# Where the embedding's projection waits in SBUF: places for all sixteen tiles, stores after x has landed, squares of x ahead of copies

## The chip, the core and the metric

The kernel runs on one core of a Trainium2 chip. The metric is the device time of one execution in microseconds (us), as the median of several runs. A second source is one profiled execution, of which every instruction's start and duration is known; its own time stands beside its span below.

## What is computed

One layer of a decoder trunk on a sequence of 512 positions and 2048 channels, in float32. Cut to what matters here:

```python
h = rms_norm(x, norm_g)                    # x: (512, 2048)
proj = h @ w_in                            # queries, keys, values, gates, ...
kc = compress(k_c, pe_k, w1_k, w2_k)       # k_c, v_c: slices of proj
vc = compress(v_c, pe_v, w1_v, w2_v)
o_a = attention(q, kc, vc, k_s, v_s, k_w, v_w, gates) * silu(z_a)
o_b = spatial_gating(uv, ...) * silu(z_b)
merged = g_a * (o_a @ w_up_a) + g_b * (o_b @ w_up_b)
x = x + merged @ w_out
x = x + sigmoid(x @ w_ple_gate) * (p @ w_ple)    # p: (512, 256), w_ple: (256, 2048)
return rms_norm(x, final_g)
```

The product `p @ w_ple` depends on nothing else, so the kernel computes it first, while x is on its way, and stores it in DRAM until the last stage. It is "the embedding's projection" of the title.

## The kernel before

All matrix products run through one generator, `gemm()`, over a list of jobs. A float32 matrix is split into a high part (ScalarE, line 98, or line 100 with a scale) and a low part (VectorE, line 104 or 106), and each product is three matmuls: high by high, low by high, high by low. Weights come in loads of 512 KB (`load_to`, line 138, on SyncE's queue) into three rotating buffers `raw`; each load holds two sub-tiles, which are split into `hi` (four buffers) and `lo` (three). A load is issued only when its buffer is free, and everything behind it on SyncE's queue waits with it. `fill(n)` advances the generator by n groups of three matmuls, so the order of each engine's instructions is written out by hand and is the order of the program's lines.

The jobs of interest are the first ones. `pl0` to `pl3` are the projection of the embedding: each has eight groups of three matmuls (two steps of the contraction by four blocks of 128 positions) and gives four banks of PSUM, 128 x 512 each. `evac_ple` copies them to SBUF (ScalarE at line 346 or VectorE at line 348, by a string of letters a and d for each job and block) and stores them to the DRAM tensor `spill` from GpSimd's queue (line 349), 512 KB at a time, through three rotating buffers `ple`. Then come `kc0`, `kc1`, `vc0` and `vc1`: keys and values that will be compressed (matmuls at lines 190 to 192), of which `evac_c` makes the tiles `tokk` and `tokv` (lines 327 and 328 on ScalarE, 331 and 332 on VectorE).

The start of the program (lines 555 to 642) interleaves four things by hand. `keep_busy(10)` issues ten matmuls on the identity matrix (line 576). p is transposed (line 601) and split. The four blocks of x, 1 MB each (`xt`, line 570), get their sum of squares on ScalarE (`stats`, line 579, and a square root, line 580), a reciprocal and a scaling on VectorE (`scale`, lines 583 and 584). Then `turn(k)` transposes the k-th 128 channels of all four blocks on TensorE (line 591), and `turned(k)` splits them into `act_h` and `act_l` (lines 100 and 106), the activation for all products with `w_in`. `fill` calls stand between these steps: the projection's matmuls cover the time until x is ready.

PSUM has eight banks, two for each of the letters g, s, t, o. `pl0` and `pl2` use g, g, s, s; `pl1` and `pl3` use t, t, o, o; `turn(0)` and `turn(1)` use s, `turn(2)` uses g, and `turn(3)` to `turn(5)` use s.

SBUF is given out by pools. `xin` holds x, p and the projection's buffers and closes after the last `turn`. `mid` holds the attention's values (`vt`), gates, compressed keys and the masks `b0`, `c0`, `cm`, which GpSimd makes at lines 650 to 658. `cmp` holds the compression's weights; GpSimd clears the margins of `tokk` and `tokv` (line 665) and then loads the weights (lines 668 to 673). The position terms `pek` and `pev` are transposed on TensorE at line 677, after `finish("kc1")`.

Of the kernel before, what the change touches and what calls it, by code (L numbers as in the profile page):

```python
# [12 lines left out]
F32 = mybir.dt.float32  # L13
F32R = mybir.dt.float32r
# [6 lines left out]
P = 128  # L21
S = 512
D = 2048
TT = S // P
KT = D // P
HEADS = 16
GROUPS = 4
HD = 64
NCMP = 32
# [22 lines left out]
def kernel(ctx: ExitStack, tc: tile.TileContext, x, p, norm_g, w_in,  # L52
                      pe_k, w1_k, w2_k, pe_v, w1_v, w2_v, ln_g, ln_b, sgu_w, sgu_b,
                      w_up_a, w_up_b, w_out, w_ple, w_ple_gate, final_g, out):
    nc = tc.nc
    x, out = x[0], out[0]
    p = p[0, 0]
    norm_g, w_in, ln_g, ln_b, sgu_w, sgu_b = norm_g[0], w_in[0], ln_g[0], ln_b[0], sgu_w[0], sgu_b[0]
    pe_k, w1_k, w2_k, pe_v, w1_v, w2_v = pe_k[0], w1_k[0], w2_k[0], pe_v[0], w1_v[0], w2_v[0]
# [8 lines left out]
    def bank(kind, name):  # L68
        return psum.tile([P, 512], F32, tag=kind, name=name)
# [20 lines left out]
    def flush():  # L90
        todo = list(deferred)
        deferred.clear()
        for f in todo:
            f()
# [39 lines left out]
    def load_to(i):  # L134
        while state["loads"] <= min(i, len(loads) - 1):
            job, k0, n = loads[state["loads"]]
            t = stream.tile([P, n, job.cols], F32, tag="raw", name="raw")
            nc.sync.dma_start(t, job.w[k0 * P:(k0 + n) * P, job.c0:job.c0 + job.cols]
                              .rearrange("(k p) c -> p k c", p=P))
            raw[state["loads"]] = (t, k0)  # L140
            state["loads"] += 1

    def split_to(i, more=1):
        while state["high"] <= min(i + more, len(subs) - 1):
            job, k, n, li = subs[state["high"]]
            t, k0 = raw[li]
            if k >= job.kt - job.tail:
                hi = f_tiles["th"][:, k - job.kt + job.tail:][:, :n]
            else:
                hi = stream.tile([P, n, job.cols], F32R, tag="hi", name="hi", bufs=4)  # L150
            src = t[:, k - k0:k - k0 + n]
            high(hi, src)
            parts[state["high"]] = [hi, None, src]
            state["high"] += 1
        while state["low"] <= min(i, len(subs) - 1):
            job, k, n, li = subs[state["low"]]
            pt = parts[state["low"]]
            if k >= job.kt - job.tail:
                pt[1] = f_tiles["tl"][:, k - job.kt + job.tail:][:, :n]
            else:  # L160
                pt[1] = stream.tile([P, n, job.cols], F32R, tag="lo", name="lo")
            low(*pt)
            state["low"] += 1
            li = subs[state["low"] - 1][3]
            if state["low"] == len(subs) or subs[state["low"]][3] != li:
                load_to(li + 3)
# [61 lines left out]
    def fill(n):  # L228
        for _ in range(n):
            next(run, None)  # L230

    def finish(name):
        while name not in done:
            next(run)
        flush()


    ph_ab = ExitStack()
    mid = ph_ab.enter_context(tc.tile_pool(name="mid", bufs=1))
    ph_o = ExitStack()  # L240
    o32 = None


    def h_act(k):
        return act_h[:, k], act_l[:, k]

    vt = mid.tile([P, 2, TT, GROUPS, 2 * HD], F32R, name="vt")
    gates = mid.tile([P, TT, 48], F32, name="gates")
    kc_h = mid.tile([P, GROUPS, NCMP], F32R, name="kc_h")
    kc_l = mid.tile([P, GROUPS, NCMP], F32R, name="kc_l")  # L250
    vc = mid.tile([P, GROUPS, HD], F32, name="vc")

    def kk(b, g):
        return g * 2 + b
# [81 lines left out]
    pl_in, ple_t = {}, {}  # L336
# [2 lines left out]

    def evac_ple(cg):  # L340
        def f(ps):
            for a in range(0, TT, 2):
                o = pl_in["pool"].tile([P, 2, 512], F32, tag="ple", name="ple", bufs=3)
                for t in (a, a + 1):
                    if "dddd aadd ddaa adad".split()[cg][t] == "a":
                        nc.scalar.copy(o[:, t - a], ps[t])
                    else:
                        nc.vector.tensor_copy(o[:, t - a], ps[t])
                nc.gpsimd.dma_start(spilled(cg)[:, a:a + 2], o)
        return f  # L350

    def spilled(cg):
        return spill[:, 512 * cg:512 * cg + 512].rearrange("(t p) c -> p t c", p=P)
# [200 lines left out]

    with tc.tile_pool(name="xin", bufs=4, side="right") as xin:
        xt = [xin.tile([P, D], F32, tag="xt", name=f"xt{t}") for t in range(TT)]
        pl_in["pool"] = xin
        p_nat = xin.tile([P, TT, 256], F32, name="p_nat", bufs=1)
        pl_in["h"], pl_in["l"] = ob_h[:, 0:2], ob_l[:, 0:2]
        sq = ob_h[:, 4:8].rearrange("p f t -> p (f t)")  # L560
        g_row = xin.tile([KT, P], F32, name="g_row", bufs=1)
        g_col = xin.tile([P, KT], F32, name="g_col", bufs=1)
        st = xin.tile([P, TT, 2], F32, name="st", bufs=1)
        nc.sync.dma_start(p_nat, p.rearrange("(t p) c -> p t c", p=P))
        nc.gpsimd.dma_start(g_row, norm_g.rearrange("(k p) -> k p", p=P))
        load_to(1)
        for t in range(TT):
            if t > 1:
                load_to(t)
            nc.sync.dma_start(xt[t], x[t * P:t * P + P])  # L570
        spin = bank("o", "ps_spin")

        def keep_busy(n):

            for _ in range(n):
                nc.tensor.matmul(spin[:, :P], ident, ident, start=True, stop=True)

        def stats(t):
            nc.scalar.activation(sq, xt[t], AF.Square, accum_out=st[:, t, 0:1])
            nc.scalar.activation(st[:, t, 1:2], st[:, t, 0:1], AF.Sqrt, bias=eps_t, scale=1.0 / D)  # L580

        def scale(t):
            nc.vector.reciprocal(st[:, t, 0:1], st[:, t, 1:2])
            nc.vector.tensor_scalar(out=xt[t], in0=xt[t], scalar1=st[:, t, 0:1], scalar2=None, op0=ALU.mult)

        banks = {}

        def turn(k):
            b = banks[k] = bank("ssgssstotosstoto"[k], "ps_x")
            for t in range(TT):  # L590
                nc.tensor.transpose(b[:, t * P:t * P + P], xt[t][:, k * P:k * P + P], ident)

        def turned(k):
            split(act_h[:, k], act_l[:, k], banks[k], g_col[:, k:k + 1])

        keep_busy(10)
        state["more"] = 0
        for j in range(2):
            b = bank("t", "ps_p")
            for t in range(TT):  # L600
                nc.tensor.transpose(b[:, t * P:t * P + P], p_nat[:, t, j * P:j * P + P], ident)
            split(pl_in["h"][:, j], pl_in["l"][:, j], b)
            split_to(j, 0)
        b = bank("o", "ps_g")
        nc.tensor.transpose(b[:, :KT], g_row, ident[:KT, :KT])
        split_to(3, 0)
        fill(8)
        nc.vector.tensor_copy(g_col, b[:, :KT])
        for t in range(2):
            stats(t)  # L610
            scale(t)
        split_to(5, 0)
        fill(8)
        stats(2)
        scale(2)
        split_to(7, 0)
        fill(8)
        stats(3)
        scale(3)
        split_to(8, 0)  # L620
        fill(3)
        turn(0)
        turn(1)
        turned(0)
        fill(1)
        turn(2)
        turned(1)
        fill(2)
        turn(3)
        turned(2)  # L630
        fill(2)
        for k in range(4, KT):
            turn(k)
            turned(k - 1)
            if k % 4 == 0:
                split_to(8 + k // 4, 0)
            fill(1)
        turned(KT - 1)
        state["more"] = 1
        state["ahead"] = 2  # L640
        fill(2)
        split_to(13)
    orow = ph_o.enter_context(tc.tile_pool(name="orow", bufs=1, side="right"))
    o32 = orow.tile([P, 8, S], F32, name="o32")

# [15 lines left out]
    with tc.tile_pool(name="cmp", bufs=1) as cmp:  # L661
        w1t, w2t, pet = {}, {}, {}
# [2 lines left out]
            nc.gpsimd.memset(tok[n][:, :, :, NCMP:], 0.0)  # L665
        for n, w1, w2, pe in (("k", w1_k, w2_k, pe_k), ("v", w1_v, w2_v, pe_v)):
            w1t[n] = cmp.tile([P, 16, HD], F32, name="w1" + n)
            nc.gpsimd.dma_start(w1t[n], w1.rearrange("l d e -> (l d) e").rearrange("(m p) e -> p m e", p=P))
            w2t[n] = cmp.tile([HD, 2, HD], F32, name="w2" + n)
            pet[n] = cmp.tile([NCMP, 2, HD], F32, name="pe" + n)  # L670
            for i in range(2):
                nc.gpsimd.dma_start(w2t[n][:, i], w2)
                nc.gpsimd.dma_start(pet[n][:, i], pe)
        finish("kc1")
        for n in "kv":
            b = bank("t", "ps_pe")
            nc.tensor.transpose(b[:, :NCMP], pet[n].rearrange("l i d -> l (i d)"), ident[:NCMP, :NCMP])
# [236 lines left out]
    n = len(slots)  # L914
# [40 lines left out]
    with tc.tile_pool(name="mlp", bufs=1) as mlp:  # L955
        vn = mlp.tile([P, TT, 1024], F32, name="vn")
        st = mlp.tile([P, TT, 2, 6], F32, name="bst")
# [87 lines left out]
    for cg in range(4):  # L1045
# [13 lines left out]
        for j in range(4):  # L1059
            k = 4 * cg + j  # L1060
# [3 lines left out]
            h, l = x2_act(k)  # L1064
# [31 lines left out]
```

## Time and profile before

| what | value |
|---|---|
| median of 3 runs | 1661.67 us |
| lowest and highest | 1661.51 and 1663.06 us |
| the profiled execution's own time | 1662.88 us |
| its span, first to last instruction | 1661.2 us |
| around the span | 1.68 us |
| TensorE matmul busy | 1643.5 us, 99% of the span |
| VectorE, ScalarE, GpSimd busy | 45%, 37%, 7% of the span |

A row of the timeline gives start, duration, engine, line, operation, output and inputs, and in brackets how long the engine was idle before it and what released it. PE is TensorE's matmuls and PEld its weight loads, DVE is VectorE, ACT ScalarE, POOL GpSimd, SPq SyncE's queue. Matmuls overlap in their pipeline, so the distance from start to start is their cost, not the duration. A row of the windows gives the length of a stretch, then busy time and count of the engine asked for, the clock that TensorE was granted (1.00 is full), the share of time the DMA engines were busy, and GB/s.

### The profile page before, as it was taken

What the parts mean: (1) busy time and instruction counts of PE and PEld (TensorE: products, weight loads), DVE (VectorE), ACT (ScalarE), POOL (GpSimd) and SP (SyncE); (2) the same over time, 40 slices, a digit from 0 to 9 for tenths busy, and PEclk for the clock granted to TensorE, in tenths of its full rate; (3) what the DMA queues carried; (4) which work ended last, traced back from release to release, by engine and by line L of the source; (5) the groups of instructions that cost most, each with busy time, mean ns of one, the idle gap of its engine ahead of it and who ended that gap; (6) DMA issues with size and microseconds to landing.
All of it is one profiled execution on the core that took longest, in us unless ns stands there. A gap on an engine that the chain in (4) does not pass through costs nothing.

```text
span 1661.2 us, 20583 instructions
## 1 busy us (share of the span) xinstructions
PE 1643.5 (99%) x7841; PEld 1370.3 (82%) x7841; DVE 743.5 (45%) x1486; ACT 612.6 (37%) x1229; POOL 116.9 (7%) x148
## 2 busy tenths in 40 slices
PE   8999999999999999999999999999999999999997
PEld 6878988888888888888888888888888888888886
DVE  5434358888884353343232223223223533333336
ACT  5433346667663332233222222222223422223335
POOL 2100000101110002000000000000000000000101
PEclk9999999999999999999999999999999999999999
DMA  7422421111114333333333333333333522363333
GB/s 291 130 76 74 114 77 52 39 51 51 49 54 140 101 90 89 90 98 96 99 101 90 101 100 91 102 95 96 102 91 100 202 90 89 92 225 90 102 100 128
DMA packets 217250, 168.02 MB, mean 101 GB/s; under 512 B 5040, under 2 KB 191040, under 8 KB 215616
## 3 DMA queue, kind: packets, MB, share of 16 engines
q1 hardware_dynamic: 213472, 151.57, 31.4%
q0 software_dynamic: 3536, 14.79, 2.4%
q8 instruction: 61, 1.00, 0.2%
q14 instruction: 37, 0.30, 0.1%
q10 hardware_dynamic: 144, 0.36, 0.1%
HBM read 158.31 MB, written 8.39 MB: 100 GB/s over the span
## 4 chain that ended last, share of the span: by engine, by line
PE 96%; DVE 2%; ACT 1%; DMA 0%; issue 0%; POOL 0%; DVEq 0%; POOLq 0%; ACTq 0%
PE ps_wo L198 4%; PE ps_ma L190 3%; PE ps_mb L190 3%; PE ps_wo L199 3%; PE ps_mb L191 3%; PE ps_ma L192 3%; PE ps_ma L191 3%; PE ps_wo L200 3%; PE ps_mb L192 3%; PE ps_pg L198 3%; PE ps_pg L200 3%; PE ps_pg L199 3%; PE ps_t L802 2%; PE ps_za L190 2%; PE ps_za L192 2%; PE ps_za L191 2%
## 5 line engine op out<-in xcount | busy, mean ns | idle before, releaser
L104 DVE TENSOR_TENSOR lo<-raw,hi 128x512 fp32r<-128x512 f32 (+1 forms) x536 | 366.6, 687 | 639.1 <-PE ps_mb L192 127.4
L98 ACT CAST hi<-raw 128x512 fp32r<-128x512 f32 (+1 forms) x536 | 328.1, 615 | 723.8 <-PE ps_wo L200 99.0
L198 PE MATMUL ps_wo<-hi,act_h 128*128 128x512 f32 x256 | 101.0, 395 | 0.1
L200 PE MATMUL ps_wo<-hi,act_l 128*128 128x512 f32 x256 | 99.8, 390 | 0.0
L199 PE MATMUL ps_wo<-lo,act_h 128*128 128x512 f32 x256 | 99.7, 390 | 0.0
L190 PE MATMUL ps_ma<-act_h,hi 128*128 128x512 f32 x256 | 99.6, 389 | 0.0
L191 PE MATMUL ps_ma<-act_l,hi 128*128 128x512 f32 x256 | 99.6, 389 | 0.0
L192 PE MATMUL ps_ma<-act_h,lo 128*128 128x512 f32 x256 | 99.6, 389 | 0.0
L190 PE MATMUL ps_mb<-act_h,hi 128*128 128x512 f32 x256 | 99.6, 389 | 0.0
L191 PE MATMUL ps_mb<-act_l,hi 128*128 128x512 f32 x256 | 99.6, 389 | 0.0
L192 PE MATMUL ps_mb<-act_h,lo 128*128 128x512 f32 x256 | 99.6, 389 | 0.0
L98 ACT CAST pth<-ps_t 128x512 fp32r<-128x512 f32 (+1 forms) x88 | 48.0, 546 | 65.6 <-PE ps_t L802 65.3
L763 ACT ACTIVATE prob<-prob,st 128x512 f32<-128x512 f32 (+3 forms) x128 | 70.7, 555 | 4.0 <-DVE st L754 3.8
L453 POOL TENSOR_TENSOR m<-sig,sig 128x512 f32<-128x512 f32 x16 | 27.0, 1690 | 582.3 <-DVE sig L451 464.1
L104 DVE TENSOR_TENSOR ptl<-ps_t,pth 128x512 fp32r<-128x512 f32 (+1 forms) x88 | 56.2, 639 | 21.3 <-ACT pth L98 20.4
L754 DVE CUSTOM_DVE_ANT_0 prob<-ps_s,b 128x512 f32<-128x512 f32 (+3 forms) x128 | 56.3, 486 | 10.1 <-PE ps_s L751 9.8
L200 PEld LDWEIGHTS ps_wo<-hi,act_l 128*128 128x128 f32 x256 | 48.1, 188 | 10.3
L198 PEld LDWEIGHTS ps_wo<-hi,act_h 128*128 128x128 f32 x256 | 48.1, 188 | 10.2 <-DVE sig L451 0.5
L192 PEld LDWEIGHTS ps_ma<-act_h,lo 128*128 128x128 f32 x256 | 48.0, 188 | 10.0
L192 PEld LDWEIGHTS ps_mb<-act_h,lo 128*128 128x128 f32 x256 | 48.0, 188 | 10.0
L190 PEld LDWEIGHTS ps_mb<-act_h,hi 128*128 128x128 f32 x256 | 48.0, 188 | 10.0
L191 PEld LDWEIGHTS ps_ma<-act_l,hi 128*128 128x128 f32 x256 | 48.0, 188 | 10.0
(316 smaller groups left out, 3684.3 us busy)
## 6 DMA issues: line engine op xcount, KB each, us to landing
raw<-in_w_in_dram SPq DMA_DIRECT2D x164, 512.0 KB, 3.5
raw<-in_w_out_dram SPq DMA_DIRECT2D x32, 512.0 KB, 3.6
raw<-in_w_ple_gate_dram SPq DMA_DIRECT2D x32, 512.0 KB, 3.5
raw<-in_w_up_a_dram SPq DMA_DIRECT2D x16, 512.0 KB, 3.7
raw<-in_w_up_b_dram SPq DMA_DIRECT2D x16, 512.0 KB, 3.7
xt<-in_x_dram SPq DMA_DIRECT2D x4, 1024.0 KB, 10.8
spill<-ple POOLq DMA_DIRECT2D x8, 512.0 KB, 5.6
m<-in_x_dram POOLq DMA_DIRECT2D x4, 1024.0 KB, 7.5
```

Of the source, the lines that this page charges most:

```text
L98: nc.scalar.copy(hi, src)
L104: nc.vector.tensor_tensor(out=lo, in0=src, in1=hi.bitcast(F32), op=ALU.subtract)
L190: nc.tensor.matmul(ps, hi[:, j], ah, start=st, stop=False)
L191: nc.tensor.matmul(ps, hi[:, j], al, start=False, stop=False)
L192: nc.tensor.matmul(ps, lo[:, j], ah, start=False, stop=sp)
L198: nc.tensor.matmul(o, ah[:, sl], hi[:, j], start=st, stop=False)
L199: nc.tensor.matmul(o, ah[:, sl], lo[:, j], start=False, stop=False)
L200: nc.tensor.matmul(o, al[:, sl], hi[:, j], start=False, stop=sp)
L453: nc.gpsimd.tensor_tensor(out=merge_tiles["m"][:, f], in0=merge_tiles[0], in1=t, op=ALU.add)
L754: nc.vector.tensor_tensor_reduce(out=pt[:, j * n:j * n + n], in0=o[:, j], in1=b0[:, 512 - n:], scale=-SLOPE[h], scalar=3.0e38, op0=ALU.add ...
L763: nc.scalar.activation(sl, sl, AF.Exp, bias=st[:, 0, j, hh:hh + 1], scale=-1.0, accum_out=st[:, 1, j, hh:hh + 1])
L802: nc.tensor.transpose(b[:, (2 * e + hh) * P:(2 * e + hh + 1) * P], pts[hh][:, c:c + P], ident)
```

## The change

- The projection's result gets one SBUF tile of 128 x 4 x 4 x 512 with a place for every one of the sixteen blocks, where three rotating buffers of two blocks were.
- The stores to `spill` leave `evac_ple`: four of 1 MB each are issued together, after the last group of `pl3`. Ahead of them on GpSimd stands a copy of one column of `st` into a new tile `order`.
- The copies' engines: `pl1` goes from ScalarE, ScalarE, VectorE, VectorE to VectorE for all four blocks; `pl2` from VectorE, VectorE, ScalarE, ScalarE to ScalarE for all four, in the order 2, 3, 0, 1. `pl0` and `pl3` stay.
- `stats(2)` moves ahead of the `fill(8)` of `pl1`, so its squares stand ahead of what follows on ScalarE; `stats(3)` and `scale(3)` move ahead of the `fill(8)` of `pl2`.
- The load of `w_ple` for `pl3` leaves its place ahead of x's last block on SyncE's queue and stands behind it.
- Eight matmuls on the identity where ten were. Of `pl3`, two groups instead of three stand ahead of `turn(0)`, and three instead of two behind `turn(3)`.
- The pool `mid` and its tiles are opened after `xin` is closed.
- The loads of `pek` and `pev` stand ahead of the other compression weights, and their transposes follow `vc0` instead of `kc1`.

```diff
--- before.py
+++ after.py
@@ -236,19 +236,12 @@
 
 
     ph_ab = ExitStack()
-    mid = ph_ab.enter_context(tc.tile_pool(name="mid", bufs=1))
     ph_o = ExitStack()
-    o32 = None
+    mid = o32 = None
 
 
     def h_act(k):
         return act_h[:, k], act_l[:, k]
-
-    vt = mid.tile([P, 2, TT, GROUPS, 2 * HD], F32R, name="vt")
-    gates = mid.tile([P, TT, 48], F32, name="gates")
-    kc_h = mid.tile([P, GROUPS, NCMP], F32R, name="kc_h")
-    kc_l = mid.tile([P, GROUPS, NCMP], F32R, name="kc_l")
-    vc = mid.tile([P, GROUPS, HD], F32, name="vc")
 
     def kk(b, g):
         return g * 2 + b
@@ -339,14 +332,12 @@
 
     def evac_ple(cg):
         def f(ps):
-            for a in range(0, TT, 2):
-                o = pl_in["pool"].tile([P, 2, 512], F32, tag="ple", name="ple", bufs=3)
-                for t in (a, a + 1):
-                    if "dddd aadd ddaa adad".split()[cg][t] == "a":
-                        nc.scalar.copy(o[:, t - a], ps[t])
-                    else:
-                        nc.vector.tensor_copy(o[:, t - a], ps[t])
-                nc.gpsimd.dma_start(spilled(cg)[:, a:a + 2], o)
+            o = pl_in["out"][:, cg]
+            for t in ((0, 1, 2, 3), (2, 3, 0, 1))[cg % 4 == 2]:
+                if "dddd dddd aaaa adad".split()[cg][t] == "a":
+                    nc.scalar.copy(o[:, t], ps[t])
+                else:
+                    nc.vector.tensor_copy(o[:, t], ps[t])
         return f
 
     def spilled(cg):
@@ -554,20 +545,21 @@
 
     with tc.tile_pool(name="xin", bufs=4, side="right") as xin:
         xt = [xin.tile([P, D], F32, tag="xt", name=f"xt{t}") for t in range(TT)]
-        pl_in["pool"] = xin
+        pl_in["out"] = xin.tile([P, 4, TT, 512], F32, name="ple", bufs=1)
         p_nat = xin.tile([P, TT, 256], F32, name="p_nat", bufs=1)
         pl_in["h"], pl_in["l"] = ob_h[:, 0:2], ob_l[:, 0:2]
         sq = ob_h[:, 4:8].rearrange("p f t -> p (f t)")
         g_row = xin.tile([KT, P], F32, name="g_row", bufs=1)
         g_col = xin.tile([P, KT], F32, name="g_col", bufs=1)
         st = xin.tile([P, TT, 2], F32, name="st", bufs=1)
+        order = xin.tile([P, 1], F32, name="order", bufs=1)
         nc.sync.dma_start(p_nat, p.rearrange("(t p) c -> p t c", p=P))
         nc.gpsimd.dma_start(g_row, norm_g.rearrange("(k p) -> k p", p=P))
         load_to(1)
         for t in range(TT):
-            if t > 1:
-                load_to(t)
             nc.sync.dma_start(xt[t], x[t * P:t * P + P])
+            if t == 1:
+                load_to(2)
         spin = bank("o", "ps_spin")
 
         def keep_busy(n):
@@ -593,7 +585,7 @@
         def turned(k):
             split(act_h[:, k], act_l[:, k], banks[k], g_col[:, k:k + 1])
 
-        keep_busy(10)
+        keep_busy(8)
         state["more"] = 0
         for j in range(2):
             b = bank("t", "ps_p")
@@ -610,15 +602,16 @@
             stats(t)
             scale(t)
         split_to(5, 0)
+        stats(2)
         fill(8)
-        stats(2)
         scale(2)
+        stats(3)
         split_to(7, 0)
+        scale(3)
+        nc.gpsimd.tensor_copy(order, st[:, 3, 0:1])
         fill(8)
-        stats(3)
-        scale(3)
         split_to(8, 0)
-        fill(3)
+        fill(2)
         turn(0)
         turn(1)
         turned(0)
@@ -628,7 +621,9 @@
         fill(2)
         turn(3)
         turned(2)
-        fill(2)
+        fill(3)
+        for cg in range(4):
+            nc.gpsimd.dma_start(spilled(cg), pl_in["out"][:, cg])
         for k in range(4, KT):
             turn(k)
             turned(k - 1)
@@ -640,6 +635,12 @@
         state["ahead"] = 2
         fill(2)
         split_to(13)
+    mid = ph_ab.enter_context(tc.tile_pool(name="mid", bufs=1))
+    vt = mid.tile([P, 2, TT, GROUPS, 2 * HD], F32R, name="vt")
+    gates = mid.tile([P, TT, 48], F32, name="gates")
+    kc_h = mid.tile([P, GROUPS, NCMP], F32R, name="kc_h")
+    kc_l = mid.tile([P, GROUPS, NCMP], F32R, name="kc_l")
+    vc = mid.tile([P, GROUPS, HD], F32, name="vc")
     orow = ph_o.enter_context(tc.tile_pool(name="orow", bufs=1, side="right"))
     o32 = orow.tile([P, 8, S], F32, name="o32")
 
@@ -665,13 +666,15 @@
             nc.gpsimd.memset(tok[n][:, :, :, NCMP:], 0.0)
         for n, w1, w2, pe in (("k", w1_k, w2_k, pe_k), ("v", w1_v, w2_v, pe_v)):
             w1t[n] = cmp.tile([P, 16, HD], F32, name="w1" + n)
-            nc.gpsimd.dma_start(w1t[n], w1.rearrange("l d e -> (l d) e").rearrange("(m p) e -> p m e", p=P))
             w2t[n] = cmp.tile([HD, 2, HD], F32, name="w2" + n)
             pet[n] = cmp.tile([NCMP, 2, HD], F32, name="pe" + n)
             for i in range(2):
+                nc.gpsimd.dma_start(pet[n][:, i], pe)
+        for n, w1, w2 in (("k", w1_k, w2_k), ("v", w1_v, w2_v)):
+            nc.gpsimd.dma_start(w1t[n], w1.rearrange("l d e -> (l d) e").rearrange("(m p) e -> p m e", p=P))
+            for i in range(2):
                 nc.gpsimd.dma_start(w2t[n][:, i], w2)
-                nc.gpsimd.dma_start(pet[n][:, i], pe)
-        finish("kc1")
+        finish("vc0")
         for n in "kv":
             b = bank("t", "ps_pe")
             nc.tensor.transpose(b[:, :NCMP], pet[n].rearrange("l i d -> l (i d)"), ident[:NCMP, :NCMP])
```

## The prediction

> **What bounds the kernel now.** I read the page's busy times and chain first, then the chain of waits of the first 90 us, then the timelines of each engine from 17 to 46 us, since all edits lie in the start of the program.
>
> ```profile
> PE 1643.5 (99%) x7841; PEld 1370.3 (82%) x7841; DVE 743.5 (45%) x1486; ACT 612.6 (37%) x1229; POOL 116.9 (7%) x148
> ...
> PE 96%; DVE 2%; ACT 1%; DMA 0%; issue 0%; POOL 0%; DVEq 0%; POOLq 0%; ACTq 0%
> ```
>
> TensorE is the bound: 96% of the chain is its own work. What an edit can bring is TensorE's idle or slow time, and 1661.2 - 1643.5 = 17.7 us is all the idle there is. The chain of the start, in order of time (start, duration, what), leaves TensorE once for long:
>
> ```profile
> 18.24 0.60 ACT ple L346
> ...
> 19.13 7.11 DMA spill<-ple
> 26.32 1.08 ACT ple L346 x2
> 27.40 1.91 ACT ob_h L579 x2
> 29.33 0.30 ACT st L580
> 29.85 1.30 DVE xt L584
> 31.20 1.33 PE ps_x L591 x5
> ```
>
> A store of the projection takes 7.11 us to land; only then is its `ple` buffer free for ScalarE's copies at 26.32; only after them, ScalarE being in order, come the squares of x's last block, then its scaling, then the transpose. TensorE's rows show what that costs, and the windows show the clock beside it (the three figures after TensorE's count are clock, DMA share, GB/s):
>
> ```profile
> 8.64 0.50 PE L199 MATMUL ps_pl<-lo,ob_h 128*128 128x512 f32 x1 [0.30 <-DVE lo L104]
> ...
> 25.55 0.50 PE L199 MATMUL ps_pl<-lo,ob_h 128*128 128x512 f32 x1 [0.32 <-DVE lo L104]
> ...
> 27.51 0.49 PE L591 MATMUL ps_x<-ident,xt 128*128 128x128 f32 x3
> 31.20 1.33 PE L591 MATMUL ps_x<-ident,xt 128*128 128x128 f32 x5 [3.20 <-DVE xt L584]
> ...
> 35.73 0.63 PE L198 MATMUL ps_pl<-hi,ob_h 128*128 128x512 f32 x1
> 36.16 0.63 PE L199 MATMUL ps_pl<-lo,ob_h 128*128 128x512 f32 x1
> ...
> 36.99 0.60 PE L591 MATMUL ps_x<-ident,xt 128*128 128x128 f32 x4
> ...
> 37.90 0.40 PE L200 MATMUL ps_pl<-hi,ob_l 128*128 128x512 f32 x1
> 38.13 0.40 PE L198 MATMUL ps_pl<-hi,ob_h 128*128 128x512 f32 x1
> ...
> 38.82 0.60 PE L591 MATMUL ps_x<-ident,xt 128*128 128x128 f32 x4
> ```
>
> ```profile
> 30.00:31.00 1.00, 0.00 (x0) 0.56 1.07 422
> ...
> 36.50:37.00 0.50, 0.50 (x3) 0.55 0.00 0
> ```
>
> Three transposes of `turn(0)` run, the fourth needs the last block and waits 3.20 us. In that gap the clock falls to half (0.56 over the slice from 30 to 31), and it comes back only at about 36.95 (0.55 over the half slice before 37.00). Between, matmuls stand 0.43 us apart (35.73 to 36.16) where 0.23 is the step at full clock (37.90 to 38.13). So the store's landing is paid twice: once as idle, once as a slow clock.
>
> **The stall, term by term.** (1) Idle at 31.20: 3.20 us. (2) From 31.20 to 36.99 TensorE starts nine transposes and nine matmuls. At full clock a transpose steps by about 0.09 to 0.11 (four from 38.82 take 0.36 to the next instruction), so they are worth 9 x 0.11 + 9 x 0.23 = 3.1 us; they took 5.79, so the clock cost 2.7. (3) Idle of 0.32 at 25.55 on a `lo` of `pl3`, which VectorE made late because its own copies waited for a store; gone with it.
>
> **Does the last block come in time now?** Three things must hold: its data, ScalarE's turn, VectorE's turn.
>
> ```profile
> 4.12 0.47 SPq L570 DMA_DIRECT2D xt<-in_x_dram  x1
> 9.82 0.38 SPq L138 DMA_DIRECT2D raw<-in_w_ple_dram  x1
> 10.24 0.47 SPq L570 DMA_DIRECT2D xt<-in_x_dram  x1
> ```
>
> Time from issue to landing, in the answers on DMA for these three in order, and for the slowest store:
>
> ```profile
> xt<-in_x_dram SPq DMA_DIRECT2D x1, 1024.0 KB, 12.4
> ...
> raw<-in_w_ple_dram SPq DMA_DIRECT2D x1, 512.0 KB, 8.0
> ...
> xt<-in_x_dram SPq DMA_DIRECT2D x1, 1024.0 KB, 11.7
> ...
> spill<-ple POOLq DMA_DIRECT2D x1, 512.0 KB, 9.2
> ```
>
> Before, the third block lands at 16.5, the load for `pl3` at 17.8, the last block at 21.9, slowed by stores that run beside it. The load waits on SyncE's queue for a buffer until 9.82 and holds the last block behind it. Now the last block is issued right behind the third, at about 4.6, and no store runs until its squares are done. At the rate of the load (512 KB in 1.3 us) it lands at 16.5 + 2.6 = 19.1; at worst at the old 21.9. I take 19.1, the rate of the row next to it. The load follows at 20.4 and must be in by ScalarE's split of it, below.
>
> ```profile
> 15.06 1.13 ACT L98 CAST hi<-raw 128x512 fp32r<-128x512 f32 x2
> ...
> 17.64 1.29 DVE L104 TENSOR_TENSOR lo<-raw,hi 128x512 fp32r<-128x512 f32 x2
> 22.22 1.29 DVE L348 COPY ple<-ps_pl 128x512 f32<-128x512 f32 x2 [3.29 <-DMA spill<-ple]
> 23.42 0.15 DVE L583 RECIPROCAL st<-st 128x1 f32<-128x1 f32 x1
> 23.61 1.29 DVE L584 TENSOR_SCALAR xt<-xt,st 128x2048 f32<-128x2048 f32 x1
> ```
>
> ScalarE: free at 16.2, squares of block 2 from 16.5 (squares and root take 27.40 to 29.63, 2.2 us) to 18.7, of block 3 from 19.1 to 21.3, then two `hi` of `pl3`, 1.13, to 22.4. It then stands ready for `pl2`'s four copies. VectorE: `lo` of `pl2` end at 18.9; four copies of `pl1`, which wait for no store now, 2.6, to 21.5; reciprocal and scaling of block 2, 1.45, to 23.0; two `lo` of `pl3`, 1.3, to 24.3; block 3, 1.45, to 25.7. TensorE comes to `turn(0)` at 27.51 less one group (0.7) less the idle of 0.32, 26.5. So 0.8 us is left, and the fourth transpose comes 0.3 later still. If TensorE starts earlier (next part), VectorE's row moves with it, because `pl0`'s copies stand at its head. The old landing at 21.9 would bring `pl3`'s first `lo` and the scaling late by 1 to 1.5 us each, partly after each other: a rival below.
>
> PSUM: `turn(0)` and `turn(1)` now wait for ScalarE's copies of `pl2`'s blocks 2 and 3, which are put first for that. Each ends a copy's time (0.6) after its last matmul, and six matmuls of `pl3` (1.4 us) stand between: nothing. With all sixteen copies without a store to wait for, what is next late is the fifth transpose group, which waited 0.4 for `act_l` and still will.
>
> **The start of the program.**
>
> ```profile
> 1.43 4.64 PE ps_spin L576 x20
> ...
> 5.86 1.22 PE L601 MATMUL ps_p<-ident,p_nat 128*128 128x128 f32 x8
> ...
> 6.68 0.59 ACT L98 CAST ob_h<-ps_p 128x512 fp32r<-128x512 f32 x1 [4.38 <-PE ps_p L601]
> ```
>
> ```profile
> 0.81 0.44 SPq L564 DMA_DIRECT2D p_nat<-in_p_dram  x1
> ...
> p_nat<-in_p_dram SPq DMA_DIRECT2D x1, 512.0 KB, 4.1
> ```
>
> (The first row is the chain's, the others the timelines'.) Ten filler matmuls are twenty rows at 0.21 to 0.23 us, the slow clock's step. Two fewer bring the transposes of p forward by four rows, 0.85, to 5.0, where p is in (0.81 + 4.1 = 4.9). The first four run at the slow step, so ScalarE starts 0.6 earlier, and the projection with it. Before this was worth nothing, the stall swallowed it; now it is on the path: 0.6. Bounds: 0, if the split of the first weights sets the start, and 0.85.
>
> Of the clock the Trainium skill, "TensorE: Matmul & The Clock Gate", section "Part 1: The HAM clock gate", says that it rises only after a window of about 3.4 us in which TensorE was busy, and that the windows run free of the kernel's start. By that rule fewer fillers may leave no whole busy window ahead of the gaps between 7 and 8.6 us, and the estimate by its figure is a rise 3.4 us later, about 1.5 us lost. The trace neither confirms nor denies it for eight fillers; its rise after the stall (5.75 us of work from 31.20) is slower than the rule's least, and prices the rival below.
>
> **What moves off the path.** GpSimd's four stores carry the same 4 MB. The first two go out when `order` has read the last block's reciprocal, about 24; the last at about 32.5, when `pl3` is copied. They run beside the `w_in` loads, as before. The masks of `mid`, and with them the clearing of `tokk`, now wait for all stores and for the last `act_l`:
>
> ```profile
> 54.10 0.16 POOL L665 MEMSET tokk<- 128x64 f32 x1 [10.89 <-DVE act_l L106]
> ...
> 56.02 0.37 ACT L327 COPY tokk<-ps_kc 64x256 f32<-64x256 f32 x1 [1.22 <-PE ps_kc L192]
> ```
>
> The clearing already waited for that `act_l`; the masks, 2 us of GpSimd's work, now stand behind the wait too and push the weight loads 2 us against TensorE's stream, where `pek` and `pev` go first and are needed only after `vc0`, some 20 us later: nothing. ScalarE's copy to `tokk` at 49.0 (56.02 less 7.0) now needs the fourth store landed. At twice the slowest 512 KB, 18.4, it lands at 50.9: at most 1.9 late, with at least one split sub-tile ahead (the program splits up to two ahead; 12 x 0.23 = 2.8 us of TensorE). I take 0.
>
> **The sum.** 3.20 + 2.7 + 0.32 + 0.6 = 6.8. A second count, from the first back-to-back matmul: 95 steps of 0.23 and sixteen transposes from 8.05 reach `turn(4)` at 31.5 to 31.7, where it stood at 38.82: 7.2. I take 7.0. Span 1661.2 - 7.0 = 1654.2, and with the 1.68 us around it 1655.9 for a profiled execution. The runs of before spread from 1661.51 to 1663.06 with the profiled one, 1662.88, at the upper end. If its 1.2 us over the median lies in the length of the slow clock, which is gone now, the median falls to 1655.9; if it is the profile's own cost, to 1654.7. I forecast 1655.5.
>
> **The rivals.**
> (a) The last block is still late, 0.10. For: 0.8 us is a thin margin, and 25.7 rests on five steps. If it lands at 21.9, squares end at 24.1, the first `lo` of `pl3` at 25.4 (1.3 idle) and the scaling at 27.5 (0.5 more): some 1.8 us, no fall of the clock. 1657.3.
> (b) The clock rises late at the start, 0.08. If work counts only from 8.05 and the rise takes the 5.75 us it took after the stall, matmuls step by 0.43 until 13.8: 5.75 x (1 - 0.23/0.43) = 2.7 lost. 1658.2. Against: TensorE is still busy from 1.43 to about 7 without a gap.
> (c) The change does not free the path, 0.04: some wait that the trace of before cannot show holds the squares where they were, and the clock falls again. About 1661.
> (d) Slower, 0.04: kc0's evacuation. ScalarE and VectorE stand in order behind the wait for the fourth store, and no split passes them. Once the prepared sub-tile is used TensorE idles, and beyond about 3 us its clock falls as at 30 us. It loses what is won, and 3.3 more, when the store lands after about 60, 27 us after its issue; then 1665. Against: 9.2 is the longest of eight half-size stores.
>
> **How the numbers follow.** The forecast has 0.74 and its own range is 1654.2 to 1656.8 (the larger sum with the lower start; half of rival (a)'s delay). To hold 8 in 10 the range takes in (a) and reaches to (b): 1653.9 to 1658.2. A measurement of this kernel tells 0.2%, 3.3 us, from no change: faster means under 1658.3. Forecast, (a) and (b) are faster, 0.92, of which 0.01 is taken off for the edge of (b); (c) and that edge give 0.05 within; (d) 0.04 slower.
>
> **What would show it.** Right: no store in the chain of the start; squares of the last block at about 19 to 21.5; a clock of 1.00 in every slice from 26 to 40; no idle before the transposes over 0.5; `turn(4)` near 31.7; from there each row some 7 us earlier than before, with the same gaps. Wrong: a wait of TensorE on `xt` over 1 us, (a); steps of 0.43 in `pl0`, (b); ScalarE's `tokk` waiting for a store, (d).

## The result, and the profile after

The changed kernel takes 1655.7 us (median of 6 runs, 1655.33 to 1657.22) where the kernel before takes 1661.6 (6 runs, 1660.14 to 1663.06): ratio 0.9964, 95% interval 0.9951 to 0.9977, 5.9 us less. The forecast was 1655.5. The profiled execution has a span of 1653.6 us and a time of 1655.33, the shortest of the six. One execution of the kernel before, in the experiments, took 1819.91 us at a mean granted clock of 0.85; it is in no ratio and in no heap below.

The page's busy times, and the chain of waits of the first 60 us (start, duration, what):

```profile
PE 1639.1 (99%) x7837; PEld 1367.1 (83%) x7837; DVE 742.8 (45%) x1486; ACT 612.9 (37%) x1229; POOL 114.0 (7%) x145
```

```profile
1.30 4.97 DMA raw<-in_w_ple_dram
6.29 0.63 ACT hi L98
6.94 0.70 DVE lo L104
7.68 0.50 PE ps_pl L199
...
25.42 0.88 PE ps_x L583 x8
...
31.38 0.69 DVE ple L340
32.07 0.67 DVE act_l L106
32.88 0.63 PE ps_x L583 x4
```

No store is left in it, and no square of x. From 7.68 on it is TensorE's own work up to one short detour over VectorE at 31.38. TensorE's busy time fell too, by 4.4 us: 1.2 of that is the fillers' row (3.42 for 4.64), because there are two fewer and because they step faster towards their end; most of the rest is work that no longer runs at half clock. The timelines show the last block of x in time (ScalarE, VectorE, TensorE):

```profile
19.23 1.93 ACT L571 ACTIVATE ob_h<-xt 128x2048 fp32r<-128x2048 f32 x1
...
23.42 2.25 ACT L338 COPY ple<-ps_pl 128x512 f32<-128x512 f32 x4 [0.81 <-PE ps_pl L200]
```

```profile
17.99 2.48 DVE L340 COPY ple<-ps_pl 128x512 f32<-128x512 f32 x4
20.38 0.15 DVE L575 RECIPROCAL st<-st 128x1 f32<-128x1 f32 x1
...
23.51 1.30 DVE L576 TENSOR_SCALAR xt<-xt,st 128x2048 f32<-128x2048 f32 x1
```

```profile
7.68 0.50 PE L199 MATMUL ps_pl<-lo,ob_h 128*128 128x512 f32 x1 [0.22 <-DVE lo L104]
...
25.26 1.04 PE L583 MATMUL ps_x<-ident,xt 128*128 128x128 f32 x8
...
31.18 0.60 PE L583 MATMUL ps_x<-ident,xt 128*128 128x128 f32 x4
...
32.88 0.63 PE L583 MATMUL ps_x<-ident,xt 128*128 128x128 f32 x4 [0.40 <-DVE act_l L106]
```

The scaling ends at 24.81; the eight transposes of `turn(0)` and `turn(1)` start at 25.26 without a gap. `turn(4)` is at 31.18, where it stood at 38.82: 7.64 us earlier, and the span is 7.6 us shorter, so the rest of the program moved along unchanged. The median gained only 5.9: the profile of before is 1.3 us above its median of 1661.6, and this one is 0.4 below its own. The experiments show what sets these distances.

### The profile page after: what moved, and what is told of

It reads as the page before. It is cut to its first block, busy times and chain, and to the rows that moved or that the text cites. A ratio compares the mean times of both kernels' runs of the same rounds, so it can differ in the third digit from the quotient of the medians.

```text
span 1653.6 us, 20567 instructions
## 1 busy us (share of the span) xinstructions
PE 1639.1 (99%) x7837; PEld 1367.1 (83%) x7837; DVE 742.8 (45%) x1486; ACT 612.9 (37%) x1229; POOL 114.0 (7%) x145
## 4 chain that ended last, share of the span: by engine, by line
PE 97%; DVE 2%; ACT 1%; DMA 0%; issue 0%; DVEq 0%; SPq 0%; ACTq 0%
PE ps_wo L198 4%; PE ps_wo L200 4%; PE ps_mb L191 4%; PE ps_ma L191 4%; PE ps_ma L190 4%; PE ps_mb L192 4%; PE ps_mb L190 4%; PE ps_ma L192 4%; PE ps_wo L199 4%; PE ps_pg L198 3%; PE ps_pg L199 3%; PE ps_pg L200 3%; PE ps_t L805 2%; PE ps_za L190 2%; PE ps_za L192 2%; PE ps_za L191 2%
## 5 line engine op out<-in xcount | busy, mean ns | idle before, releaser
L190 PEld LDWEIGHTS ps_ma<-act_h,hi 128*128 128x128 f32 x256 | 48.1, 188 | 10.0
L191 PEld LDWEIGHTS ps_mb<-act_l,hi 128*128 128x128 f32 x256 | 48.1, 188 | 9.9
```

Source lines behind the costliest of these rows:

```text
L190: nc.tensor.matmul(ps, hi[:, j], ah, start=st, stop=False)
L191: nc.tensor.matmul(ps, hi[:, j], al, start=False, stop=False)
```

## Experiments

**The kernel before, again.** The same program, to read its scatter.

> The kernel before, unchanged, to read its own scatter (1660.1 to 1663.1 in six runs). Theory: the scatter is the length of the half-clock stretch behind the stall, so the runs' mean granted clock falls with their time; a stretch about 3.4 us longer costs about 1.7 us and lowers the mean clock by about 0.001. Rival: the scatter comes from the DMAs, and the mean clock is the same in short and long runs. Either way a median of 1661 to 1662.

Median 1661.56, ratio 0.9999 (0.999 to 1.0008). Together with the runs of before that stood beside three of these groups, 70 executions fall into three heaps: 25 from 1659.7 to 1660.7 (median 1660.2, mean granted clock 0.9986), 38 from 1661.2 to 1662.1 (1661.7, 0.9976), 7 from 1662.9 to 1663.1 (1663.0, 0.9960). The 16 runs of before in the fourth group fall into the same three (5, 5 and 6, from 1659.8 to 1663.2). This execution's profile is of the first heap, 1660.22:

```profile
31.19 0.77 PE L591 MATMUL ps_x<-ident,xt 128*128 128x128 f32 x5 [2.97 <-DVE xt L584]
```

```profile
30.00:31.00 1.00, 0.00 (x0) 1.00 1.11 420
31.00:32.00 1.00, 0.81 (x6) 1.00 1.03 422
```

Nearly the same idle, 2.97 for 3.20, and no fall of the clock (the figure after the count, 1.00). The execution profiled for the prediction, 1662.88, was of the slowest heap. So the scatter is the clock's: the rival, equal clocks in short and long runs, falls.

**Kept busy through the gap.** In the kernel before:

```diff
         fill(3)
+        spin = bank("g", "ps_spin")
+        keep_busy(14)
         turn(0)
```

> The kernel before with 14 extra matmuls on the identity (28 rows of 0.11 us, 3.1 us) in the gap ahead of turn(0), so that TensorE is kept at work while it waits for the last block of x. Theory: the slow steps after the gap are only the clock, and it now stays full: about 2.7 us less than before, 1659, the transposes still released at about 31.2, matmul steps of 0.23 from 31 to 37. Rival: the slow steps come from traffic of the stores or loads at that time; then 1661.6 and steps of 0.43 as before.

Median 1660.1 (1659.72 to 1660.41), ratio 0.999 (0.9981 to 0.9999).

```profile
31.04 0.77 PE L591 MATMUL ps_x<-ident,xt 128*128 128x128 f32 x5 [0.17 <-DVE xt L584]
```

```profile
31.00:32.00 1.00, 0.96 (x7) 1.00 0.98 401
```

The transposes are released as late as before, the clock stays full, and the two slower heaps are gone: all ten runs lie in the first one. The slow steps were the clock alone. Keeping it full is worth 2.8 us against the profiled execution, of which 2.7, as forecast, lie between the release and the fifth transposes (6.65 us for 9.32), but 1.5 at the median. The 1659 that was named took the 2.7 off the median, and is missed by 1.1.

**Places alone.** The kernel before with enough buffers:

```diff
-  o = pl_in["pool"].tile([P, 2, 512], F32, tag="ple", name="ple", bufs=3)
+  o = pl_in["pool"].tile([P, 2, 512], F32, tag="ple", name="ple", bufs=8)
```

The pool `mid` is opened after `xin` for it, since the two don't fit beside each other.

> The kernel before with eight buffers for the projection instead of three (and the pool of values opened after x's is closed, to make room): no copy waits for a store, and nothing else is changed: stores at once, order of squares and copies, loads and ten fillers as before. Theory: ScalarE's two copies of pl2 then wait for TensorE until about 25.9, the last block's scaling ends at about 29.7, and TensorE idles some 1.9 us instead of 3.2; 1.6 us less than before if the clock still falls, 4.3 less if it does not: 1657.3 to 1660. Rival: the wait for the store was all of it; then about 6.3 less, 1655.4, and no idle ahead of the fourth transpose.

Median 1660.27 (1658.43 to 1661.13), ratio 0.9993 (0.9984 to 1.0002): 1.35 less than the runs beside it, not clear of no change, and 0.3 above the range that was named. ScalarE and TensorE:

```profile
24.68 1.27 ACT L340 COPY ple<-ps_pl 128x512 f32<-128x512 f32 x2 [2.27 <-PE ps_pl L200]
25.84 1.92 ACT L573 ACTIVATE ob_h<-xt 128x2048 fp32r<-128x2048 f32 x1
```

```profile
29.75 0.77 PE L585 MATMUL ps_x<-ident,xt 128*128 128x128 f32 x5 [2.06 <-DVE xt L578]
```

The copies wait for no store any more, but for TensorE itself, 2.27 us, and the squares stand behind them. 1.9 us of idle was forecast, 2.06 is left. The rival, that the store was all of it, falls. The clock stays full in this profile, of a run of 1659.29, but not in every run, it seems: the three with a mean clock of 0.997 took 1660.48 to 1661.13, the other seven 1658.43 to 1660.38.

**Squares back behind the copies.** In the changed kernel:

```diff
-        stats(3)
         split_to(7, 0)
-        scale(3)
-        nc.gpsimd.tensor_copy(order, st[:, 3, 0:1])
         fill(8)
+        stats(3)
+        scale(3)
+        nc.gpsimd.tensor_copy(order, st[:, 3, 0:1])
```

> The changed kernel with the squares and scaling of the last block put back behind pl2's four copies. Theory: ScalarE, in order, waits for TensorE's pl2 until 23.4, copies until 25.6, squares until 27.9; scaling ends at about 29.4; TensorE, at turn(0) at about 25.5, idles 3.7 us and the clock may fall again: 3.7 more without the fall, 5.4 to 6.4 more with it, 1659.4 to 1662. Rival: places and deferred stores are what counts, and the order is worth under 1 us: under 1656.7.

Median 1661.26 (1661.12 to 1662.24), ratio to before 1.0002 (0.9993 to 1.0011): 5.6 us are given back, the whole change, and inside the range that was named.

```profile
29.65 1.33 PE L583 MATMUL ps_x<-ident,xt 128*128 128x128 f32 x5 [3.72 <-DVE xt L576]
```

```profile
28.00:29.00 1.00, 0.00 (x0) 0.96 0.00 0
29.00:30.00 1.00, 0.35 (x2) 0.50 0.00 0
...
35.00:36.00 1.00, 1.00 (x7) 0.63 1.02 389
```

3.72 idle, as forecast, and the clock falls at 28.9 and rises at 35.7.

**Order of squares alone.** The kernel before with three buffers, stores at once, its loads, letters and ten fillers, and one edit:

```diff
+        stats(2)
         fill(8)
-        stats(2)
         scale(2)
+        stats(3)
         split_to(7, 0)
+        scale(3)
         fill(8)
-        stats(3)
-        scale(3)
```

> The kernel before with the order of squares alone: stats(2) ahead of the fill(8) of pl1, stats(3) and scale(3) ahead of the fill(8) of pl2, and nothing else (three buffers, stores at once, loads, letters and ten fillers as before). Theory A (the order of the squares is the edit that counts, and the places only spare the copies a wait that nobody on the path then feels): the last block lands at about 21.9 as before, its squares end at 24.2, VectorE's two copies of pl1 still wait for a store until 22.2 to 23.5, and the scaling ends at about 27.5, when TensorE reaches the fourth transpose at about 27.8: idle under 0.5, no fall of the clock, 1655.9 to 1657. Theory B (both are needed, since VectorE's copies, which wait for stores, stand ahead of the scaling): TensorE idles 1.5 us or more, 1657.5 to 1660.

Median 1657.31 (1657.07 to 1658.32), ratio 0.9976 (0.9967 to 0.9986): 4.5 us of the 5.9 come from moving three calls.

```profile
22.05 1.92 ACT L579 ACTIVATE ob_h<-xt 128x2048 fp32r<-128x2048 f32 x1 [1.93 <-DMA xt<-in_x_dram]
...
27.05 1.08 ACT L346 COPY ple<-ps_pl 128x512 f32<-128x512 f32 x2 [1.63 <-DMA spill<-ple]
```

```profile
27.71 1.13 PE L591 MATMUL ps_x<-ident,xt 128*128 128x128 f32 x8
```

The last block still lands at 22.0, and a copy still waits 1.63 for a store, but the squares are ahead of it, and TensorE has no idle over 0.46 from 9 to 46 us. Theory A is right in kind; 1657.3 lies 0.3 outside its range. Its span is 1.9 us longer than the changed kernel's, and 1.2 of that is the start: the first back-to-back matmul stands at 8.89 in this profile, and at 7.68 in that one.

**Stores at once.** In the changed kernel `nc.gpsimd.dma_start(spilled(cg), o)` stands at the end of `evac_ple` again, and the late stores and `order` are gone.

> The changed kernel with each 1 MB store issued as soon as its four copies are emitted, with no wait for x. Theory: the stores of pl0 and pl1 run from about 14 beside the last block of x and delay it from 19.2 to between 20.5 and 22; its scaling ends 1.3 to 2.8 later than 24.8, and TensorE idles 0.5 to 2 us ahead of turn(0): 1656.2 to 1657.7. Rival: the order of the stores is without effect, since no copy waits for them: 1655.7.

Median 1655.72 (1655.55 to 1656.07): the rival, no effect. The expected mechanism failed: the squares of the last block still start at 19.39, since its transfer is issued at 4.4, and the first store, issued at 14.32, has moved only 0.03 of its 1 MB by 19.3, when the block is in. What comes late is the load of `pl3`:

```profile
22.95 1.14 ACT L98 CAST hi<-raw 128x512 fp32r<-128x512 f32 x2 [1.22 <-DMA raw<-in_w_ple_dram]
```

```profile
26.34 0.77 PE L584 MATMUL ps_x<-ident,xt 128*128 128x128 f32 x5 [0.24 <-DVE xt L577]
```

The stores' queue moves 1 MB between 19.3 and 23, and the load lands at 22.9 instead of 20.5. That eats the slack and 0.24 us.

**The load of `pl3` ahead of the last block.** `if t == 1: load_to(2)` becomes `if t in (1, 2): load_to(t + 1)`.

> The changed kernel with the load for pl3 put back ahead of the last block of x on SyncE's queue. Theory: the last block is issued at about 9.3 instead of 4.4 and lands one load later, at 20.5 instead of 19.2; its scaling ends at about 26, and TensorE idles 0.2 to 0.6: 1656 to 1656.3. Rival: slack takes it all, 1655.7; or the queue's late issue costs more than one load, and the wait is over 1 us.

Median 1655.91 (1655.83 to 1656.16). The last block's squares start at 20.47 instead of 19.23 (20.5 and 19.2 were named), and TensorE waits 0.25. The median lies between the theory's 1656 and the rival's 1655.7 and decides nothing; the trace shows the wait.

**Ten fillers.** `keep_busy(10)` in the changed kernel.

> The changed kernel with ten fillers instead of eight. Theory: with the stall gone the start is on the path, and two fillers at the slow step put the projection's first matmuls off by 0.6 to 0.85 us: about 1656.4. Rival: the split of the first weights, which land at 6.3, sets the start, and nothing changes: 1655.7; or the longer unbroken start raises the clock more surely, and the longest runs (1657.2) go: the same or less.

Median 1655.78 (1655.36 to 1656.0): no cost that shows in five runs, the rival. In its profile the first back-to-back matmul stands at 7.74, beside 7.68:

```profile
5.14 1.04 PE L593 MATMUL ps_p<-ident,p_nat 128*128 128x128 f32 x8
...
7.74 0.50 PE L199 MATMUL ps_pl<-lo,ob_h 128*128 128x512 f32 x1 [0.31 <-DVE lo L104]
```

The clock rose early in both, so two fillers cost 0.45 (5.14 for 4.69, where the changed kernel's transposes of p start), and that is hidden behind the first weights, which land at 6.27.

It is otherwise where the clock rises late. In the profiles of two versions below, both with eight fillers ("stores twice" and "the fifth transposes"), TensorE's step changes from 0.21 to 0.11 only at about 6, and the first back-to-back matmul comes later:

```profile
8.11 0.50 PE L199 MATMUL ps_pl<-lo,ob_h 128*128 128x512 f32 x1 [0.31 <-DVE lo L104]
```

```profile
8.06 0.50 PE L199 MATMUL ps_pl<-lo,ob_h 128*128 128x512 f32 x1 [0.25 <-DVE lo L104]
```

In the two profiles of the kernel before, with ten fillers and the same late rise, it stands at 8.48 and 8.64. So two fillers are worth about 0.06 us with an early rise, and an estimated 0.4 to 0.6 with a late one, though these kernels differ in more than the fillers.

**Four fillers.** `keep_busy(4)`.

> The changed kernel with four fillers instead of eight: TensorE is idle from about 3.2 until p lands at 4.6 to 4.9. Nothing of the data comes sooner. Theory (the clock rises after a stretch of unbroken work, so an early gap puts the rise off): matmul steps of 0.43 at the start of pl0 until somewhere from 9 to 13.5, a loss of 0.7 to 2.7 us, 1656.4 to 1658.4. Rival: the fillers do nothing, the projection's own matmuls raise the clock in time: 1655.7.

Median 1657.58 (1657.01 to 1658.12): 1.9 us slower than the changed kernel, and inside the theory's range.

```profile
4.95 1.97 PE L593 MATMUL ps_p<-ident,p_nat 128*128 128x128 f32 x8 [1.45 <-DMA p_nat<-in_p_dram]
```

```profile
9.08 0.63 PE L198 MATMUL ps_pl<-hi,ob_h 128*128 128x512 f32 x1
9.51 0.63 PE L199 MATMUL ps_pl<-lo,ob_h 128*128 128x512 f32 x1
```

A gap of 1.45 us, and the matmuls step by 0.43 up to the one at 12.49, by 0.23 from 12.86 on. The clock column of the windows reads 1.00 all through this stretch, and the run's mean clock is 0.999: of a slow start only the steps tell.

**Stores twice.** The changed kernel issues its four stores a second time.

> The changed kernel with all four stores issued twice (8 MB instead of 4; the same data to the same place): prices the new wait of GpSimd's masks and of kc0's evacuation for the last store. Theory: the last store lands at about 49 to 50 instead of 39, the copies to tokk come 2 to 4 us later than 48.5, and the sub-tiles split ahead (about 5 us of TensorE) hide it: 1655.7, no new idle of TensorE. Rival: what ScalarE waits comes out of TensorE, 2 to 4 us: 1658 to 1660.

Median 1655.71 (1655.52 to 1655.83).

```profile
51.65 0.56 POOL L653 IOTA b<- 128x512 f32 x1 [11.65 <-DMA spill<-ple]
```

```profile
51.66 0.36 ACT L320 COPY tokk<-ps_kc 64x256 f32<-64x256 f32 x1 [2.16 <-PE ps_kc L192]
```

The masks and `tokk` start together when the last store is in, 3.2 us later than the 48.48 of the changed kernel; 2 to 4 were named. (The row names TensorE as the releaser; that both engines start within 0.01 us points to the store.) TensorE has no idle between 45 and 60 us: the split sub-tiles cover it.

**The fifth transposes.** In the changed kernel `turned(3)` is emitted ahead of the last group of `pl3`:

```diff
         turned(2)
-        fill(3)
+        fill(2)
+        turned(3)
+        fill(1)
...
             turn(k)
-            turned(k - 1)
+            if k > 4:
+                turned(k - 1)
```

> The changed kernel with the split of x's fourth 128 channels, turned(3), emitted ahead of the last group of pl3 instead of behind it and its copies. Theory: the 0.40 us that TensorE still waits for act_l ahead of turn(5) goes, and the kernel is 0.4 faster: 1655.3, within the scatter of a median but plain in the trace. Rival: the copies of pl3, now later, hold a bank and give the time back: 1655.7 or more.

Median 1655.07 (1654.68 to 1655.2), ratio to before 0.9964 (0.995 to 0.9977). In its timeline TensorE has no wait at all from 8.06 to 46 us. All five runs lie below all six of the changed kernel, and below all five of the stores issued twice, which ran beside them (1655.71): the fastest version of the study, by some 0.6 us.

**Both orders in the kernel before.** The order of squares and that of `turned(3)`, with three buffers and stores at once.

> The same, with turned(3) emitted ahead of the last group of pl3 as well. Theory: 0.4 less than the kernel with the order of squares alone, the wait of 0.40 ahead of turn(5) gone. Rival: pl3's copies, which now follow turned(3) and still need a buffer of the three, come late and give it back.

Median 1656.84, 0.5 below the order of squares alone, but scattered from 1656.14 to 1659.51. Nothing shows what sets the longest runs, as its one profile is of a short one.

## Why the prediction was right, point by point

- **The stall.** The idle of 3.20 is gone, and the 0.32 at 25.55. So is the slow clock.
- **The last block.** Landing was forecast for 19.1 and squares to 21.3; the squares start at 19.23. The scaling was forecast to end at 25.7, 0.8 us ahead of `turn(0)` at 26.5 and 1.1 ahead of the fourth transpose; it ends at 24.81, 0.45 ahead of 25.26 and some 0.75 ahead of the fourth. The stores at once and the old place of the load each use that up and show 0.24 and 0.25 of wait: the margin was as thin as rival (a) said, and what crosses it costs little.
- **Term (2), the clock, was mis-sized for the median.** 2.7 is right for the profiled execution (2.7 by the kernel that was kept busy too) but 1.5 at the median, as the heaps of the kernel before show. The prediction left open whether the 1.2 us between profile and median were the clock's or the profile's own; they are the clock's.
- **The idle terms were a little small.** From start to start, the fourth transpose came 3.4 us late before, not 3.20, and the step at 25.55 cost 0.6, not 0.32, since a row's idle counts from the end of the matmul before it. With the 2.7 of the clock and 0.96 at the first back-to-back matmul (7.68 for 8.64) these make up the 7.64 at `turn(4)` but for rounding; the prediction took 7.0.
- **Luck in the number.** The sum was 0.6 short on the profiled execution, which took 1655.33 where 1655.9 was worked out; and 1655.33 is the shortest of six, 0.4 below their median. The two nearly cancel, and 1655.5 was a choice between two cases, of which the one that holds said 1655.9.
- **The start, 0.6, holds only in part.** In the pair of profiles the start gained 0.96, but an early rise of the clock would have given nearly all of that to ten fillers too (7.74). With a late rise two fillers are worth an estimated 0.4 to 0.6, about what the term says. The median with ten fillers shows no cost. The lower bound named, that the first weights' split sets the start, is what holds when the clock rises early.
- **Rival (b)** has its mechanism, at four fillers: 1.9 of the 2.7 us named. At eight, one run of six took 1657.22. Its mean clock is 0.997, where the ten runs with four fillers have 0.998 or 0.999 although they start slowly; that speaks for a half-clock stretch later in the program rather than for (b). No trace of that run exists, so it stays open.
- **Rival (d)**: the wait is there. With the stores issued twice ScalarE does stand for the store, but 3.2 us of that are covered.
- **What the prediction did not say**: which edit does the work. It called the store's landing the cause. The chain names the wait that ended last, 7.11 us of store, but behind it stood another of nearly the same end, TensorE's `pl2`. Taking the store away alone uncovers that one and brings 1.35; the order of the squares brings 4.5 with the stores as they were; without the last block's squares in their new place all other edits together bring nothing. So the prediction's chain had a real wait, but not the one that had to go; its sum stood because the change moves the squares as well.

## What to carry to other kernels

Where a chain shows a step behind a wait on an engine in order, ask whether the step needs to stand behind it at all, before making the wait shorter: moving the squares ahead of the copies brought 4.5 us, the buffers alone 1.35, which is not clear of nothing. Before a sum is set against a median, ask in which of the program's modes the one profiled execution ran, on both sides of the change; several runs with their mean granted clocks tell. A short gap of TensorE may be paid again as slow clock, and filler matmuls of no use otherwise take that part back.

## What the runs showed of the hardware that was not expected

The same idle of about 3 us costs the clock in some executions and not in others. Where it fell, it stayed at half for 6.8 us both times: from 30.1 to 36.95 before, from 28.9 to 35.7 with the squares put back. The heaps lie 1.5 and 1.3 us apart. The falls also keep step with the start: TensorE's step changes from 0.21 to 0.11 at about 6.2 before and at about 5.0 with the squares put back, and both falls come 23.9 us after that. The Trainium skill, "TensorE: Matmul & The Clock Gate", section "Part 1: The HAM clock gate", has windows of 3.413 us that run free of the kernel's start; by that figure two windows are 6.83, which the traces agree with, and one window at half clock is an estimated 1.6 us (3.413 x (1 - 0.23/0.43)), near the distance of the heaps. In the first heap's execution the step changes at about 5.95, so 23.9 us later is an estimated 29.8: of its idle, from 28.2 to 31.2, 1.6 us lie ahead of that moment, where the execution of the slowest heap had 2.1 ahead of its fall. That the phase of these windows is what sorts the executions is argued from three profiles, not shown: no run could set it.
